# Moving the evacuation of an attention accumulator from the end of a step to its middle

## The chip, the core and the metric

The kernel runs on one core of a Trainium2 chip. The metric is the device time of one execution in microseconds (us). The engines are named as the profile names them: PE is TensorE (PEld its weight loads), ACT is ScalarE, DVE is VectorE, POOL is GpSimd, SP is SyncE, which issues the DMAs.

## The reference

It is one inference step of a two-layer encoder for a prompt of 2048 tokens and a sample of 64, at a width of 1024. Both layers have the form h + RMSNorm(W_out(gated mixer(RMSNorm(h)))). Layer 0 mixes by latent attention and by a banded attention; the change does not touch it. Layer 1 is a sliding-window attention with 16 query heads and 2 key heads of 64, in chunks of 64 tokens: a chunk reads itself and the two chunks before it, and each head has a sink logit in its softmax.

```python
def _c_layer(h, pos, cache, pre_g, post_g, w_in, sinks, w_out):
    ...
    q = _rope(q.reshape(b, s, C_HEADS, C_HEAD_DIM), pos, C_ROT).reshape(b, s, C_KV_HEADS, C_GROUP, C_HEAD_DIM)
    ...
        o = _band_prompt(q, k, v, C_PAST_CHUNKS, C_SCALE, sinks=sinks)
    ...
    return h + _rms((o * jax.nn.silu(g)) @ w_out, post_g), state
```

## The kernel before

Values are kept as pairs of a rounded high part and a remainder, so that a product of two is three matmuls; a *remainder* below is the DVE operation of `lo_of` (L214), which subtracts the high part from the PSUM source. It always follows the ACT copy of `copy` (L211), which makes the high part.

Five phases follow each other; `phase5` is layer 1's attention with the output projection. Its prompt part has 16 blocks of 128 queries, and each block has four **units**: (g, e) for key head g and parity e, with four query heads each. The units are worked by a loop over `step(n)`, which has three of them in hand at once. It takes the exponentials of unit n+1 (L1702 on ACT), starts the scores of unit n+2 (L1690 on PE, row maxima with the mask in L1693 on DVE), then for each of the (at most two) key blocks b of unit n transposes the probabilities (`turn`, L1711 on PE, into a tile `t` of `ps_t`, which has two buffers), copies them to `PT` (L211 on ACT), pumps the output projection of finished blocks (L964 on PE, into the only buffer of `ps_p`), and takes the remainder (L214 on DVE), which frees `t`. In the pass b = 0, behind that, it issues the value products of unit n-1 (`av`, L1718 on PE): four matmuls into `acc`, the only buffer of the pool `ps_o`. At the end of the step unit n-1 is evacuated by `out`:

```python
if (g, e) == (0, 0):
    while J.open >= 2:
        J.rest()
        pump(1)
    J.open += 1
    B.OT = ot.tile([128, 8, 128], F32, name="OT", bufs=2)
tbm = sc.tile([64, 512], F32, name="tbm", bufs=2)
copy(tbm, self.acc[64:128])
nc.vector.tensor_tensor(B.OT[e * 64:e * 64 + 64, g * 4:g * 4 + 4].rearrange("p j q -> p (j q)"),
                        self.acc[0:64], tbm, op=ALU.add)
if (g, e) == (1, 1):
    ...
    nc.vector.reciprocal(ri, B.rs)
    J.side.add(gate(B.OT, ri, B.i * 128, 128))
```

The accumulator's upper half is copied by ACT (`tbm`, L211) and added to its lower half by DVE (L1808); the next unit's products may start only then. For a block's first unit, `out` first lets at most one earlier block be open: its loop calls `J.rest()` and pumps the projection until that block's `gate` is through. `gate` runs beside the steps as a generator. It multiplies OT by the transposed reciprocals of the row sums (L1740 on PE, L1742 on DVE), by the gate (L1748 on POOL), copies the result to `MM` (L211 on ACT) and takes its remainder (L1755 on POOL, the last reader of OT, which has two buffers). `J.rest()` also drives the tails of the projection: DVE scales z by the row's norm and a gain (L995), POOL adds the residual (L1003).

For the first 8 steps a scheduler orders all engines. From n = 8 (about 2343 us of the profiled execution) the queues of PE, DVE, ACT and SP keep the order in which the code issues; POOL's order is still the scheduler's.

Of the kernel before, what the change touches and what calls it, by code (L numbers as in the profile page):

```python
# [110 lines left out]
def kernel(ctx, tc, a, o, upto=5):  # L111
# [1540 lines left out]
    def phase5():  # L1652

        with ExitStack() as st:
# [213 lines left out]
            def pump(rate):  # L1868
                if J.mm:
                    return J.pump(rate)  # L1870
                for _ in range(RATEL):
                    if next(left, left) is left:
                        return open_projections()
# [8 lines left out]
            def step(n):  # L1882
                cur, prv, nxt = us.get(n), us.get(n - 1), us.get(n + 1)
                if nxt:
                    nxt.exp([0, 1, 2, 3])
                if n + 2 < len(units):
                    us[n + 2] = Unit(*units[n + 2])
                    us[n + 2].start()
                    if n % 4 == 1 and n // 4 + 2 < 16:
                        blocks[n // 4 + 2] = Block(BLOCKS5[n // 4 + 2])  # L1890
                for b in range(2):
                    low = None
                    if cur and b < cur.B.nb:
                        PT, low = cur.turn(b * 128, 128)
                        cur.tasks.append(PT)
                    pump(RATE5 / 2)
                    if low:
                        low()
                    if b == 0 and prv:
                        prv.av()  # L1900
                if prv:
                    prv.out()
                    us.pop(n - 1)
                    if n % 4 == 0 and n // 4 + 1 in blocks and n > 0:
                        blocks[n // 4 + 1].load_values()
                if not J.loaded:
                    J.load.pump(1)
                if n >= NS5:
                    J.samp.pump(1)
                if J.made < FAST5:  # L1910
                    J.side.pump(SP5)
                J.rest()

            for n in range(NAUTO5):
                step(n)
            with manual(M5, ORDERED | {mybir.EngineType.SP}):
                for n in range(NAUTO5, len(units) + 1):
                    step(n)
                J.banks += [(ps_t, "t"), (ps_o, "acc")]
                J.dense = True  # L1920
                while J.done < 17:
                    J.side.pump(TAIL)
                    J.samp.pump(1)
                    J.rest()
                    J.last = J.done == 16
                    J.pump(4)
                J.side.drain()
                J.tails.drain()
# [104 lines left out]
```

## Time and profile before

| | |
|---|---|
| three timed runs | 2724.87, 2735.03, 2735.82 us (median 2735.03) |
| profiled execution | 2728.87 us, of which the span is 2727.1 |
| mean granted PE clock | 0.988 |
| last slices, PE busy of 40 us: 2400 to 2440 / 2560 to 2600 / 2600 to 2640 | 38.47 / 38.47 / 39.01 us |
| DVE busy in the same | 33.68 / 34.96 / 34.33 us |
| ACT busy in the same | 33.03 / 31.40 / 30.82 us |
| matmul L1718, mean of one | 401 ns |

A row of the timeline has its start in us from the span's start, its length in us, the engine, the line, the operation, what it writes and reads (128x512 is partitions by elements), and how many instructions of a kind were merged into it. A bracket tells how long the engine stood idle before it, and which operation ended that. In a row of groups, the busy time in us and the mean in ns stand behind the first bar, the idle time and what ended it behind the second.

### The profile page before, as it was taken

The numbers are of one execution on the slowest core, as the hardware profiler recorded it, in microseconds if no ns is written. First come the engines' busy times: TensorE is split into PE (matmuls) and PEld (weight loads), VectorE is DVE, ScalarE is ACT, GpSimd is POOL, SyncE is SP. The second block draws the span as 40 slices with busy tenths as digits, with TensorE's granted clock in tenths as the row PEclk, the third lists the DMA queues.
The fourth block names the chain that finished last, engine by engine and source line by source line (L and its number), as shares of the span: only waits on it lengthen the run. The fifth ranks groups of instructions, "written<-read, shape, count | busy, mean of one in ns | idle before, by whom it ended". The sixth has DMA issues, their size and how long they took to land. (4 is left out here: it accounts for less than half of the span.)

```text
span 2727.1 us, 46654 instructions
## 1 busy us (share of the span) xinstructions
PE 2566.5 (94%) x16296; PEld 2337.6 (86%) x16296; DVE 1568.7 (58%) x4255; ACT 1392.4 (51%) x3548; POOL 522.1 (19%) x1110
## 2 busy tenths in 40 slices
PE   7999999999999999999888999799999999999997
PEld 6999999899988888888777887679999998787886
DVE  5453345352237778787667766466223214787886
ACT  4332232422337777777666665452233223877783
POOL 0001000001002323211101333342001000344443
PEclk9999999999999999999999999999999998999999
DMA  7546444727447666651666766466425428455552
GB/s 239 171 147 209 133 143 129 255 96 234 143 118 200 194 170 188 167 155 48 194 187 167 204 191 172 149 216 224 149 96 169 127 72 246 109 139 133 137 132 70
DMA packets 382282, 437.92 MB, mean 161 GB/s; under 512 B 49936, under 2 KB 308888, under 8 KB 378816
## 3 DMA queue, kind: packets, MB, share of 16 engines
q1 hardware_dynamic: 382048, 434.95, 54.2%
q8 instruction: 129, 2.11, 0.3%
q14 instruction: 105, 0.86, 0.1%
HBM read 282.80 MB, written 157.09 MB: 161 GB/s over the span
## 5 line engine op out<-in xcount | busy, mean ns | idle before, releaser
L237 PE MATMUL pm<-X,W 128*128 128x384 f32 (+2 forms) x4536 | 752.8, 324 | 2.5 <-DVE ev L214 1.7
L237 PEld LDWEIGHTS pm<-X,W 128*128 128x128 f32 x4536 | 730.4, 189 | 6.2 <-DVE ev L214 2.3
L211 ACT ACTIVATE PT<-t 128x512 fp32r<-128x512 f32 (+3 forms) x704 | 344.5, 504 | 268.9 <-PE t L1203 113.6
L214 DVE SCALAR_TENSOR_TENSOR PT<-t,PT 128x512 fp32r<-128x512 f32 (+3 forms) x688 | 376.0, 569 | 100.8 <-ACT PT L211 99.3
L964 PE MATMUL proj<-Wo,MM 128*128 128x512 f32 (+1 forms) x1416 | 391.6, 407 | 11.3 <-ACT z L211 8.1
L964 PEld LDWEIGHTS proj<-Wo,MM 128*128 128x128 f32 (+1 forms) x1416 | 246.1, 187 | 59.5 <-ACT z L211 11.6
L214 DVE SCALAR_TENSOR_TENSOR ev<-pm,ev 128x256 fp32r<-128x256 f32 (+3 forms) x197 | 98.6, 502 | 336.9 <-ACT ev L430 102.2
L237 PE MATMUL pm<-W,X 128*128 128x256 f32 (+5 forms) x2040 | 281.2, 297 | 0.0
L237 PEld LDWEIGHTS pm<-W,X 128*128 128x128 f32 (+1 forms) x2040 | 272.0, 187 | 1.0
L702 ACT ACTIVATE P<-s,m 128x512 f32<-128x512 f32 (+9 forms) x344 | 209.3, 616 | 33.3 <-DVE m L691 30.7
L683 PE MATMUL s<-KA,Q 128*128 128x512 f32 (+7 forms) x640 | 201.1, 396 | 10.5 <-ACT P L702 8.4
L228 DVE TENSOR_TENSOR W<-R,W 128x768 fp32r<-128x768 f32 (+3 forms) x114 | 116.0, 1055 | 134.0 <-ACT W L227 133.7
L726 PE MATMUL t<-ident,P 128*128 128x128 f32 x1088 | 176.3, 276 | 3.4 <-ACT P L702 1.0
L689 DVE TENSOR_REDUCE m<-s 128x1 f32<-128x480 f32 (+7 forms) x216 | 132.4, 613 | 80.3 <-PE s L683 79.9
L726 PEld LDWEIGHTS t<-ident,P 128*128 128x128 f32 x1088 | 134.6, 141 | 41.7 <-ACT P L702 15.1
L754 PE MATMUL acc<-PT,V 128*128 128x256 f32 x1152 | 156.3, 285 | 6.6 <-DVE OT L763 6.6
L754 PEld LDWEIGHTS acc<-PT,V 128*128 128x128 f32 x1152 | 140.6, 188 | 12.0 <-PE t L726 6.0
L1702 ACT ACTIVATE P<-s,m 128x256 f32<-128x256 f32 (+2 forms) x264 | 119.4, 465 | 11.6 <-DVE m L1694 10.3
L1216 PE MATMUL acc<-PT,V 128*128 128x256 f32 x672 | 111.6, 298 | 13.7 <-DVE OT L1226 11.0
L1180 DVE CUSTOM_DVE_ANT_0 s<-s,bias 128x640 f32<-128x640 f32 (+4 forms) x128 | 95.4, 745 | 42.9 <-PE s L1176 40.7
L1693 DVE CUSTOM_DVE_ANT_0 s<-s,mask 128x256 f32<-128x256 f32 (+1 forms) x256 | 107.6, 422 | 20.2 <-PE t L1711 10.9
L683 PE MATMUL s<-KR,Q 128*128 128x384 f32 (+6 forms) x320 | 116.2, 363 | 0.6 <-DMA Q<-sQR 0.6
(248 smaller groups left out, 3927.7 us busy)
## 6 DMA issues: line engine op xcount, KB each, us to landing
Q<-sQA SPq DMA_DIRECT2D x128, 128.0 KB, 3.3
sWO<-W SPq DMA_DIRECT2D x32, 512.0 KB, 3.8
Q<-sQB SPq DMA_DIRECT2D x128, 128.0 KB, 3.1
Wo<-sWO SPq DMA_DIRECT2D x16, 1024.0 KB, 8.8
Q<-sQC SPq DMA_DIRECT2D x32, 512.0 KB, 7.7
R<-in_ab_w_in_dram SPq DMA_DIRECT2D x40, 384.0 KB, 4.1
K<-sKB SPq DMA_DIRECT2D x56, 256.0 KB, 5.6
V<-sVB SPq DMA_DIRECT2D x24, 512.0 KB, 6.7
```

Of the source, the lines that this page charges most:

```text
L211: nc.scalar.activation(out, in_, AF.Copy)
L214: nc.vector.scalar_tensor_tensor(out, x, scale, hi, op0=ALU.mult, op1=ALU.subtract)
L228: nc.vector.tensor_tensor(Wv[:, 1, k0:k1], Rv, Wv[:, 0, k0:k1], op=ALU.subtract)
L237: nc.tensor.matmul(ps, lhs(x, k), rhs(y, k), start=(j == 0), stop=(j == n - 1))
L683: nc.tensor.matmul(s[:r, :n], self.Q[:, x, self.qo:self.qo + r], rhs, start=(x == 0), stop=(x == 2))
L689: nc.vector.tensor_reduce(m[:r, j:j + 1], s[:r, :n], axis=AX.X, op=ALU.max)
L702: nc.scalar.activation(self.P[:r, o0:o0 + n], self.s.pop(j)[:r, :n], AF.Exp, bias=self.m[:r, 6:7], accum_out=acc)
L726: nc.tensor.transpose(t[:, b], self.P[:, (b0 + b) * 128:(b0 + b + 1) * 128], ident)
L754: nc.tensor.matmul(acc[:, (i // 2) % 2], H.V[:, b0 + b], PT[:, x, b], start=(b0 + b == 0 and x == 0), stop=(b0 + b == i and x == 1))
L964: nc.tensor.matmul(p, M[:, x, k, :r], W[k][:, y, cs], start=(k == k0 and t == 0), stop=(k == k1 - 1 and t == 2))
L1216: nc.tensor.matmul(acc, self.H.V[:, self.base - self.H.b0 + b], self.PT[:, x, off + b], start=(b == 0 and x == 0), stop=(b == nblk - 1 and ...
L1702: nc.scalar.activation(self.P[:, c, :w], self.s[:, c, :w], AF.Exp, bias=m[:, 1, c:c + 1], accum_out=m[:, 0, c:c + 1])
```

## The change

The call of `out` moves from the step's end into the pass b = 0, directly behind `av`. With it move the loop of a block's first unit, the reciprocal, and the start of `gate` of its last.

```diff
                         low()
                     if b == 0 and prv:
                         prv.av()
+                        prv.out()
                 if prv:
-                    prv.out()
                     us.pop(n - 1)
                     if n % 4 == 0 and n // 4 + 1 in blocks and n > 0:
                         blocks[n // 4 + 1].load_values()
```

The order of the built programs differs only from step 8 on. SP's order is the same throughout, and POOL's main operations keep theirs but for small ones on row sums.

*The step that evacuates a block's last unit (1, 1).* On DVE, between the row maxima of the unit started and the first operation of `gate` of the block before, there stood before:

```order
L1694 SCALAR_TENSOR_TENSOR m<-m,nsink 128x4
L214 SCALAR_TENSOR_TENSOR PT<-t,PT 128x512 x2
L1808 TENSOR_TENSOR OT<-acc,tbm 64x512
L1812 RECIPROCAL ri<-rsum 128x16
L1742 TENSOR_TENSOR OT<-OT,t 128x512
```

And now:

```order
L1694 SCALAR_TENSOR_TENSOR m<-m,nsink 128x4
L214 SCALAR_TENSOR_TENSOR PT<-t,PT 128x512
L1808 TENSOR_TENSOR OT<-acc,tbm 64x512
L1812 RECIPROCAL ri<-rsum 128x16
L214 SCALAR_TENSOR_TENSOR PT<-t,PT 128x512
L1742 TENSOR_TENSOR OT<-OT,t 128x512
```

The addition and the reciprocal now stand between the two remainders.

*The same step and the next on ACT.* The first two rows of PT belong to the closing unit's step; behind the exponentials (L1702) begins the step that evacuates the next block's first unit (0, 0). Before:

```order
L211 ACTIVATE PT<-t 128x512 x2
L211 ACTIVATE z<-proj 128x512
L211 ACTIVATE tbm<-acc 64x512
L1702 ACTIVATE P,m<-s,m 128x256 x4
L1705 ACTIVATE m<-m 128x4
L211 ACTIVATE PT<-t 128x512
L983 ACTIVATE sq,ss_27397<-z 128x512
L211 ACTIVATE PT<-t 128x512
L211 ACTIVATE MM<-OT 128x1024
L211 ACTIVATE tbm<-acc 64x512
```

And now:

```order
L211 ACTIVATE PT<-t 128x512
L211 ACTIVATE tbm<-acc 64x512
L211 ACTIVATE PT<-t 128x512
L211 ACTIVATE z<-proj 128x512
L1702 ACTIVATE P,m<-s,m 128x256 x4
L1705 ACTIVATE m<-m 128x4
L211 ACTIVATE PT<-t 128x512
L983 ACTIVATE sq,ss_27397<-z 128x512
L211 ACTIVATE MM<-OT 128x1024
L211 ACTIVATE tbm<-acc 64x512
L211 ACTIVATE PT<-t 128x512
```

In the first step tbm passes one copy of PT and that of z; in the second, tbm and the copy of MM pass the second copy of PT.

*The step that evacuates a block's first unit (0, 0).* On DVE, from the end of the row maxima of this step to the first of the next, before:

```order
L1694 SCALAR_TENSOR_TENSOR m<-m,nsink 128x4
L214 SCALAR_TENSOR_TENSOR PT<-t,PT 128x512 x2
L995 SCALAR_TENSOR_TENSOR z<-z,rs,g_post 128x512 x2
L1808 TENSOR_TENSOR OT<-acc,tbm 64x512
L1693 ISA s,m<-s,mask 128x256
```

And now:

```order
L1694 SCALAR_TENSOR_TENSOR m<-m,nsink 128x4
L214 SCALAR_TENSOR_TENSOR PT<-t,PT 128x512
L995 SCALAR_TENSOR_TENSOR z<-z,rs,g_post 128x512 x2
L1808 TENSOR_TENSOR OT<-acc,tbm 64x512
L214 SCALAR_TENSOR_TENSOR PT<-t,PT 128x512
```

The second remainder is now behind the pair of L995 and the addition. On PE the loop's two groups of projection products go along:

```order
 L1718 MATMUL acc<-PT,VC 128x512 x4
-L1711 MATMUL t<-ident,P 128x128 x4
 L964 MATMUL proj<-Wo_25852,MM 128x512 x3
 L964 MATMUL proj<-Wo_25854,MM 128x512 x3
+L1711 MATMUL t<-ident,P 128x128 x4
 L964 MATMUL proj<-Wo_26273,MM 128x512 x3
 L964 MATMUL proj<-Wo_26275,MM 128x512 x3
```

There the second transpositions stand behind two more groups of projection products. This is PE's only difference, in twelve such steps; a first unit with only one key block (query block 0) has no second transpositions.

## The prediction

> **What bounds the kernel now.** I read the page's busy shares first, then the window of layer 1's attention grouped by line, then the timelines of TensorE and of all engines over one block.
>
> ```profile
> span 2727.1 us, 46654 instructions
> PE 2566.5 (94%) x16296; PEld 2337.6 (86%) x16296; DVE 1568.7 (58%) x4255; ACT 1392.4 (51%) x3548; POOL 522.1 (19%) x1110
> ```
>
> TensorE (PE) is busy for 94% of the span; only time in which it waits can be won. The next rows are PE's groups of 2343 to 2680 us, where the order of layer 1's steps is written by hand: count, busy time, mean, then the idle time before the group and who ended it.
>
> ```profile
> L964 PE MATMUL proj<-Wo,MM 128*128 128x512 f32 x639 | 171.0, 406 | 0.0
> L1711 PE MATMUL t<-ident,P 128*128 128x128 f32 x432 | 65.5, 275 | 2.3 <-DVE PT L214 1.1
> L1718 PE MATMUL acc<-PT,VC 128*128 128x512 f32 x216 | 60.7, 401 | 13.0 <-DVE OT L1808 13.0
> ```
>
> The value products (L1718) alone wait: 13.0 us, for the addition L1808 that empties their only accumulator. Is this spread over all steps? PE's timeline says no:
>
> ```profile
> 2383.57 0.66 PE L1711 MATMUL t<-ident,P 128*128 128x128 f32 x4 [1.09 <-DVE PT L214]
> 2405.09 1.16 PE L1718 MATMUL acc<-PT,VC 128*128 128x512 f32 x4 [0.56 <-DVE OT L1808]
> 2429.45 1.17 PE L1718 MATMUL acc<-PT,VC 128*128 128x512 f32 x4 [0.71 <-DVE OT L1808]
> 2453.81 1.17 PE L1718 MATMUL acc<-PT,VC 128*128 128x512 f32 x4 [0.71 <-DVE OT L1808]
> 2503.81 1.22 PE L1718 MATMUL acc<-PT,VC 128*128 128x512 f32 x2 [3.80 <-DVE OT L1808]
> 2673.03 1.16 PE L1718 MATMUL acc<-PT,VC 128*128 128x512 f32 x4 [1.65 <-DVE OT L1808]
> 2685.87 5.81 PE L964 MATMUL acc<-Wo,MM 128*128 128x512 f32 x24 [1.65 <-DVE OT L1808]
> ```
>
> It comes once in a block of four steps, 24.36 us apart (2429.45 to 2453.81), always after the **opening** step, which evacuates a block's first unit. The step before it, which evacuates the last unit of the block before, I call **closing**; the one after it, **following**. This is an opening step, then the following one, on all engines:
>
> ```profile
> 2420.75 0.63 DVE L1742 TENSOR_TENSOR OT<-OT,t 128x512 f32<-128x512 f32 x1
> 2421.46 2.40 POOL L1748 TENSOR_TENSOR OT<-OT,G 128x1024 f32<-128x1024 f32 x1 [4.18 <-DVE OT L1742]
> 2423.80 1.43 DVE L214 SCALAR_TENSOR_TENSOR PT<-t,PT 128x512 fp32r<-128x512 f32 x2
> 2423.91 0.60 ACT L211 ACTIVATE PT<-t 128x512 fp32r<-128x512 f32 x1 [0.93 <-PE t L1711]
> 2424.40 1.05 ACT L211 ACTIVATE MM<-OT 128x1024 fp32r<-128x1024 f32 x1
> 2425.15 3.56 DVE L995 SCALAR_TENSOR_TENSOR z<-z,rs,g_post 128x512 f32<-128x512 f32 x2
> 2425.53 2.63 POOL L1755 TENSOR_TENSOR MM<-OT,MM 128x1024 fp32r<-128x1024 f32 x1 [1.37 <-ACT MM L211]
> 2428.63 0.67 DVE L1808 TENSOR_TENSOR OT<-acc,tbm 64x512 f32<-64x512 f32 x1
> 2429.23 0.41 DVE L1693 CUSTOM_DVE_ANT_0 s<-s,mask 128x256 f32<-128x256 f32 x1
> 2430.81 1.19 PE L1690 MATMUL s<-KC,Q 128*128 128x256 f32 x8
> 2431.39 1.28 DVE L214 SCALAR_TENSOR_TENSOR PT<-t,PT 128x512 fp32r<-128x512 f32 x2
> 2432.14 0.66 PE L1711 MATMUL t<-ident,P 128*128 128x128 f32 x4
> ```
>
> The addition is late because VectorE (DVE) is: it works without a pause from L1742 to the remainders (L214) of 2431.39. Two things lengthen that stretch. First, the pair of L995 takes 3.56 us, where one usually takes 0.74:
>
> ```profile
> L995 DVE SCALAR_TENSOR_TENSOR z<-z,rs,g_post x26: 732/743/2903, 2376.0 to 2669.4; 128x512 f32<-128x512 f32 x24, 64x512 f32<-64x512 f32 x2
> 2503.07 0.68 DVE L1808 TENSOR_TENSOR OT<-acc,tbm 64x512 f32<-64x512 f32 x1 [4.79 <-POOL MM L1755]
> ```
>
> The second L995 stands still until GpSimd's L1755 ends (2428.16) and is done 0.55 later. Second, the addition needs L1755 itself, as the row of 2503.07 shows: it frees the OT buffer. So the chain of an opening step is L1742, L1748, the copy of MM, L1755, L1808; then the row maxima (L1693) and the remainder at 2431.39. That remainder is a second wait: the following step's transpositions start at 2432.14, 0.14 after the scores end (2430.81 + 1.19 = 2432.00), and need its t buffer.
>
> **The change part by part.** No instruction is added or taken out, and SP's queue is the same, so no transfer moves. What moves is the accumulator's copy (tbm, ScalarE), the addition, a closing step's reciprocal, and in an opening step two groups of projection products, now ahead of the second transpositions. All that PE does is still done: 0 us in itself.
>
> *Closing step.* These are its rows, one block later than above:
>
> ```profile
> 2440.71 1.08 PE L1718 MATMUL acc<-PT,VC 128*128 128x512 f32 x4
> 2441.63 0.60 PE L1711 MATMUL t<-ident,P 128*128 128x128 f32 x4
> 2442.27 0.60 ACT L211 ACTIVATE PT<-t 128x512 fp32r<-128x512 f32 x1 [2.14 <-PE t L1711]
> 2442.90 0.69 DVE L214 SCALAR_TENSOR_TENSOR PT<-t,PT 128x512 fp32r<-128x512 f32 x1 [0.95 <-ACT PT L211]
> 2442.97 0.60 ACT L211 ACTIVATE z<-proj 128x512 f32<-128x512 f32 x1
> 2443.59 0.59 ACT L211 ACTIVATE tbm<-acc 64x512 f32<-64x512 f32 x1
> 2444.16 0.60 PE L1711 MATMUL t<-ident,P 128*128 128x128 f32 x4
> 2444.22 0.68 DVE L1808 TENSOR_TENSOR OT<-acc,tbm 64x512 f32<-64x512 f32 x1 [0.63 <-ACT tbm L211]
> 2444.94 0.26 DVE L1812 RECIPROCAL ri<-rsum 128x16 f32<-128x16 f32 x1
> ```
>
> The products end at 2441.79; ScalarE and DVE then idle (2.14, 0.95, 0.63) for transpositions and for a copy that stands third in its queue. In the new order tbm runs at 2441.88 (an estimate: 0.09 behind the products) to 2442.47, the second PT copy to 2443.10, the addition 2442.51 to 2443.2, the reciprocal to 2443.4, the remainder 2443.4 to 2444.1. L1742 starts at 2444.05, not at 2420.75 + 24.36 = 2445.11: **1.06 us earlier** against PE. The remainder now ends at 2444.1 instead of 2443.59 and frees the buffer for transpositions at 2444.16: 0.06 are left, cost 0.
>
> *Opening step.* L1748 ends 1.06 earlier. The copy of MM no longer stands behind the second PT copy, which held it from 2423.86 to 2424.40; taking 0.50, L1755 and the addition come **1.56** earlier, at 2427.07 on the clock above. But the second remainder is now behind the addition instead of ahead of L995: +0.65 (half of 1.28). So maxima, first remainder and buffer come 1.56 - 0.65 = **0.91** earlier. The products of the following step need that second remainder only for their fourth matmul, some 0.9 us in, when it is done. The two projection groups ahead of the second transpositions cost nothing: those transpositions' PT copy and remainder are behind tbm and the addition anyhow.
>
> What does PE lose there now? Where it doesn't wait, it overlaps neighbours:
>
> ```profile
> 2432.55 2.35 PE L964 MATMUL proj<-Wo,MM 128*128 128x512 f32 x9
> 2434.73 1.10 PE L1718 MATMUL acc<-PT,VC 128*128 128x512 f32 x4
> 2443.13 1.19 PE L1690 MATMUL s<-KC,Q 128*128 128x256 f32 x8
> ```
>
> Products start 0.17 before the projection's end, transpositions 0.16 before the scores' (2444.16 against 2444.32). So an opening costs 0.71 + 0.17 at the products and 0.14 + 0.16 at 2432.14, or 1.18 us; 1.05 if the first overlap is left out. DVE gives back 0.91 of it; 0.1 to 0.3 stays as a wait of L1711 for L214.
>
> Whether the second L995 still runs into L1755 hardly matters. L1755 would be issued at 2448.33, the pair at 2447.78 and 2448.45, so the race is 0.12 us from turning; if the second wins, L1755 ends at 2451.6 and the addition starts at 2451.65 instead of 2451.45. [...]
>
> *The sum.* Thirteen openings stand in 2343 to 2680. Ten are like the one above (0.56 to 0.81 at the products): 10 x 0.91 = 9.1. The first, whose 1.09 at 2383.57 waits for the same remainder: 0.9. That of 2503.81 has no second remainder, but no second PT copy to be rid of either: 1.06 to 1.5, taken 1.3. The last (1.65) has no maxima behind it: 1.5. The end (1.65 at 2685.87) waits for a tbm that now stands ahead of a z copy: 1.3. Together **14.1 us**. The profiled execution took 2728.87 us (span 2727.1), so 2714.8. The three timed runs are 2724.87, 2735.03 and 2735.82; their median lies 6.2 above the profiled one, which puts the same gain at 2720.9. I forecast **2717**, between the two.
>
> Bounds. The idle times set the most: 12 x 1.18 + 3.8 + 1.65, about 19.5. The least, if DVE's stretch starts no earlier: 0.50 - 0.65, below nothing, taken 0 per block.
>
> **The rivals.**
> *All of it is won.* If DVE comes early enough for both waits, 19.5 go: 2709. For it: the residue is only 0.1 to 0.3. Against: the work on DVE between L1755's end and the transpositions grows by one remainder.
> *The wait changes its name.* If L1742 is not earlier (because ScalarE is not free at 2441.88), only the 0.50 of MM's copy is won and 0.65 paid; products no longer wait, the following transpositions do, by what was saved. 2729, no change. For it: DVE has no pause in the stretch. Against: the idle 2.14, 0.95 and 0.63 of the closing step, just where the moved pair lands.
> *Slower.* DVE and ScalarE take their instructions in order, so the closing step's second remainder must wait for tbm and the addition. If tbm starts as late as now, the addition at 2444.22 and the reciprocal put the remainder at 2445.1 to 2445.8, and the opening step's transpositions 1.7 us behind 2444.16. Against the 1.05 it replaces that is +0.7 in 12 blocks: 2737. It decides from a tbm 1 us later than worked out (0.06 + 0.91). [...]
>
> **How the numbers follow.** Forecast 0.55, all of it 0.10, changed name 0.27, slower 0.08. The range runs from 2706 (all of it, from the fastest timed run: 2724.87 - 19.5 = 2705.4) to 2730 (no change). About 0.5%, or 13.7 us, is what a measurement of this kernel can tell from no change, so faster means under 2721.4: most of the forecast case and all of the first rival, less what runs that differ by 11 us blur: 0.53. Same 0.42; slower 0.05, the worse part of the last rival with that blur.
>
> **What would show it.** Right: the products' wait for L1808 falls from 13.0 to under 4 us, the block's period from 24.36 to about 23.45, ACT's rows read tbm between two PT copies, L1755 starts 1.5 us earlier against PE. A new wait of L1711 for L214 of 0.1 to 0.3 a block is expected; 0.7 or more means the second rival; waits before the opening step's transpositions mean the third. Wrong altogether: waits in steps that have none now, or a z copy (L211) that PE starts to wait for.

## The result and the profile after

| | before | after |
|---|---|---|
| median of five runs | 2735.03 us (2724.87 to 2735.82) | 2710.89 us (2704.74 to 2715.87) |
| ratio, 95% interval | | 0.992 [0.9894, 0.9947] |
| span of the profiled execution | 2727.1 us | 2704.2 us |
| period of a block of four steps | 24.35 us | 23.11 us |

The change makes the kernel faster by 0.8%. In a second comparison, together with experiments, the changed kernel stood at 0.9932 [0.9915, 0.9948]. This is the head of the page of after, with the busy shares of the engines:

```profile
span 2704.2 us, 46634 instructions
PE 2562.3 (95%) x16296; PEld 2337.8 (86%) x16296; DVE 1568.3 (58%) x4255; ACT 1390.6 (51%) x3548; POOL 520.4 (19%) x1110
```

The work is the same. PE's busy time is 4.2 us shorter (2566.5 to 2562.3) and the span 22.9 us, so most of what has gone is waiting. PE's groups of 2343 to 2660 us in after (behind the last bar the idle time and what ended it):

```profile
L1711 PE MATMUL t<-ident,P 128*128 128x128 f32 x428 | 64.8, 274 | 0.4 <-DVE PT L214 0.4
L1718 PE MATMUL acc<-PT,VC 128*128 128x512 f32 x212 | 58.0, 393 | 2.4 <-DVE OT L1808 2.4
```

The products waited 13.0 us for the addition; 2.4 are left. The transpositions waited 2.3; 0.4 are left. PE's timeline in after has only these waits for the evacuation in the steps in question:

```profile
2379.34 0.66 PE L1711 MATMUL t<-ident,P 128*128 128x128 f32 x4 [0.38 <-DVE PT L214]
2493.32 0.74 PE L1718 MATMUL acc<-PT,VC 128*128 128x512 f32 x2 [2.36 <-DVE OT L1808]
2663.09 5.80 PE L964 MATMUL acc<-Wo,MM 128*128 128x512 f32 x24 [0.27 <-DVE OT L1808]
```

The 0.7 us that stood in every block are gone without a successor. The timeline of all engines in after, a closing step and the opening step behind it, shows how:

```profile
2411.04 1.08 PE L1718 MATMUL acc<-PT,VC 128*128 128x512 f32 x4
2412.22 0.59 ACT L211 ACTIVATE tbm<-acc 64x512 f32<-64x512 f32 x1 [1.77 <-PE acc L1718]
2412.84 0.68 DVE L1808 TENSOR_TENSOR OT<-acc,tbm 64x512 f32<-64x512 f32 x1 [0.56 <-ACT tbm L211]
2413.71 0.63 DVE L214 SCALAR_TENSOR_TENSOR PT<-t,PT 128x512 fp32r<-128x512 f32 x1
2414.26 0.68 DVE L1742 TENSOR_TENSOR OT<-OT,t 128x512 f32<-128x512 f32 x1
2415.01 2.41 POOL L1748 TENSOR_TENSOR OT<-OT,G 128x1024 f32<-128x1024 f32 x1 [3.05 <-DVE OT L1742]
2417.03 1.09 PE L1718 MATMUL acc<-PT,VC 128*128 128x512 f32 x4
2417.45 1.06 ACT L211 ACTIVATE MM<-OT 128x1024 fp32r<-128x1024 f32 x1 [0.51 <-POOL OT L1748]
2417.96 3.60 DVE L995 SCALAR_TENSOR_TENSOR z<-z,rs,g_post 128x512 f32<-128x512 f32 x2
2418.59 2.42 POOL L1755 TENSOR_TENSOR MM<-OT,MM 128x1024 fp32r<-128x1024 f32 x1 [0.86 <-ACT MM L211]
2421.48 0.67 DVE L1808 TENSOR_TENSOR OT<-acc,tbm 64x512 f32<-64x512 f32 x1
2423.22 1.08 PE L1718 MATMUL acc<-PT,VC 128*128 128x512 f32 x4
2424.84 0.68 DVE L214 SCALAR_TENSOR_TENSOR PT<-t,PT 128x512 fp32r<-128x512 f32 x1
2425.58 0.66 PE L1711 MATMUL t<-ident,P 128*128 128x128 f32 x4
```

Read it from the opening step's products (2417.03 here, 2422.35 before). L1755 starts 1.56 us behind them; before it was 3.18 (2425.53). The addition starts 4.45 behind them; before, 6.28. The next products (2423.22) come 1.07 us after the addition's end (2422.15), so they no longer feel it. The first remainder of the following step starts 7.81 behind them (2424.84), where it was 9.04, and the transpositions that need it (2425.58) run through.

The period can be read from the reciprocals (L1812), one in each block. Five blocks in before, then five in after:

```profile
2542.42 0.25 DVE L1812 RECIPROCAL ri<-rsum 128x16 f32<-128x16 f32 x1
2664.17 0.25 DVE L1812 RECIPROCAL ri<-rsum 128x16 f32<-128x16 f32 x1
```

```profile
2527.69 0.25 DVE L1812 RECIPROCAL ri<-rsum 128x16 f32<-128x16 f32 x1
2643.22 0.25 DVE L1812 RECIPROCAL ri<-rsum 128x16 f32<-128x16 f32 x1
```

121.75 / 5 = 24.35 and 115.53 / 5 = 23.11: **1.24 us a block**. Of the 22.9 us of the span, 2.95 stand ahead of the part with the written order, where both programs are alike: the last addition ahead of it stands at 2340.90 in before and at 2337.95 in after. That is scatter between executions. The change itself is worth the other 20 us in this pair, some 1.3 of them by TensorE's clock (last section).

### The profile page after: what moved, and what is told of

Read it like the earlier page. It is cut to its first block, busy times and chain, and to the rows that moved or that the text cites. A ratio compares the mean times of both kernels' runs of the same rounds, so it can differ in the third digit from the quotient of the medians.

```text
span 2704.2 us, 46634 instructions
## 1 busy us (share of the span) xinstructions
PE 2562.3 (95%) x16296; PEld 2337.8 (86%) x16296; DVE 1568.3 (58%) x4255; ACT 1390.6 (51%) x3548; POOL 520.4 (19%) x1110
## 5 line engine op out<-in xcount | busy, mean ns | idle before, releaser
L214 DVE SCALAR_TENSOR_TENSOR PT<-t,PT 128x512 fp32r<-128x512 f32 (+3 forms) x688 | 377.2, 568 | 78.4 <-ACT PT L211 77.2
L964 PE MATMUL proj<-Wo,MM 128*128 128x512 f32 (+1 forms) x1416 | 396.6, 410 | 10.7 <-ACT z L211 8.1
L964 PEld LDWEIGHTS proj<-Wo,MM 128*128 128x128 f32 (+1 forms) x1416 | 248.6, 188 | 58.6 <-ACT z L211 11.3
L214 DVE SCALAR_TENSOR_TENSOR ev<-pm,ev 128x256 fp32r<-128x256 f32 (+3 forms) x197 | 98.6, 503 | 338.3 <-ACT ev L430 101.1
L1702 ACT ACTIVATE P<-s,m 128x256 f32<-128x256 f32 (+2 forms) x264 | 119.3, 471 | 8.8 <-DVE m L1694 8.7
L1693 DVE CUSTOM_DVE_ANT_0 s<-s,mask 128x256 f32<-128x256 f32 (+1 forms) x256 | 107.8, 422 | 19.6 <-PE t L1711 8.5
```

Source lines behind the costliest of these rows:

```text
L214: nc.vector.scalar_tensor_tensor(out, x, scale, hi, op0=ALU.mult, op1=ALU.subtract)
L964: nc.tensor.matmul(p, M[:, x, k, :r], W[k][:, y, cs], start=(k == k0 and t == 0), stop=(k == k1 - 1 and t == 2))
L1702: nc.scalar.activation(self.P[:, c, :w], self.s[:, c, :w], AF.Exp, bias=m[:, 1, c:c + 1], accum_out=m[:, 0, c:c + 1])
```

## The experiments

The change touches all four units of a block. Which of them counts? Three theories stood at first. A: DVE's long stretch starts earlier because the *closing* unit is evacuated earlier. B: what counts is the earlier evacuation of the *opening* unit. C: each step brings its own share. Four kernels evacuate only some units in the middle of their steps:

```diff
+EARLY = ((1, 1),)
...
                     if b == 0 and prv:
                         prv.av()
+                        if (prv.g, prv.e) in EARLY:
+                            prv.out()
                 if prv:
-                    prv.out()
+                    if (prv.g, prv.e) not in EARLY:
+                        prv.out()
```

With these four, the lines behind the edit have numbers one higher (L1719 are the products, L1809 the addition, L1712 the transpositions, L215 the remainder, L1743, L1749 and L1756 the gate's three operations, L996 the z pair).

**The closing unit alone**, `EARLY = ((1, 1),)`:

> Only a block's last unit (1, 1) is evacuated in the middle of its step; the other three stay at the end. Theory A (VectorE's stretch from the gate's first product L1742 to the next remainder is the bound, and the closing step makes it start earlier): L1742 about 1.2 us earlier against PE, the block's period falls from 24.36 to 23.1-23.3 us, the time by 14-19 us against before. Theory B (PE waits for the accumulator of the block's first unit, so it is that unit's earlier evacuation that counts): period stays at 24.3-24.4, time within 3 us of before. Theory C (each of the four steps gives its share): period about 24.05, 4-6 us.

2724.63 us (2719.22 to 2733.28), ratio 0.9991 [0.9975, 1.0007] against 2729.11 of before. Period 24.35, the products still wait 0.7 in each ordinary block. Theory A is wrong as it stands. Its timeline over an opening step tells why:

```profile
2422.94 0.68 DVE L1743 TENSOR_TENSOR OT<-OT,t 128x512 f32<-128x512 f32 x1
2423.69 2.40 POOL L1749 TENSOR_TENSOR OT<-OT,G 128x1024 f32<-128x1024 f32 x1 [3.05 <-DVE OT L1743]
2425.71 1.09 PE L1719 MATMUL acc<-PT,VC 128*128 128x512 f32 x4
2427.27 0.60 ACT L212 ACTIVATE PT<-t 128x512 fp32r<-128x512 f32 x1 [1.66 <-PE t L1712]
2427.77 1.05 ACT L212 ACTIVATE MM<-OT 128x1024 fp32r<-128x1024 f32 x1
2428.90 2.62 POOL L1756 TENSOR_TENSOR MM<-OT,MM 128x1024 fp32r<-128x1024 f32 x1 [2.49 <-ACT MM L212]
2432.81 1.17 PE L1719 MATMUL acc<-PT,VC 128*128 128x512 f32 x4 [0.70 <-DVE OT L1809]
```

L1743 is earlier, by as much as with the full change: 2.77 us ahead of the products, not 1.60. L1749 is done at 2426.09. But the copy of MM stands in ScalarE's queue behind the second PT copy, which waits for PE's second transpositions (1.66) and runs at 2427.27. MM starts at 2427.77, 2.06 behind the products, as before (2424.40 - 2422.35 = 2.05). POOL idles instead (2.49), and nothing reaches PE. Two places outside the ordinary blocks gain: the long wait (3.80 in before) falls to 2.36, in a step without a second PT copy, and the wait at the end falls from 1.65 to 0.28. These 2.8 us are less than the comparison can tell from nothing.

**The opening unit alone**, `EARLY = ((0, 0),)`:

> Only a block's first unit (0, 0) is evacuated in the middle of its step. Theory A: the copy of MM gains 0.5 us, the remainder behind the addition costs 0.6, so the period stays within 0.15 us of 24.36 and the time within 4 us of before; the wait at the products gets shorter and one at the following transpositions longer. Theory B: period 23.1-23.5, 12-19 us faster. Theory C: about 24.05, 4-6 us.

2726.32 us (2721.77 to 2733.01), ratio 1.0 [0.9985, 1.0015]. Here the wait does change its name. From its timeline:

```profile
2420.29 1.09 PE L1719 MATMUL acc<-PT,VC 128*128 128x512 f32 x4
2422.99 2.42 POOL L1756 TENSOR_TENSOR MM<-OT,MM 128x1024 fp32r<-128x1024 f32 x1 [0.86 <-ACT MM L212]
2425.88 0.67 DVE L1809 TENSOR_TENSOR OT<-acc,tbm 64x512 f32<-64x512 f32 x1
2426.60 1.20 PE L1719 MATMUL acc<-PT,VC 128*128 128x512 f32 x4
2429.23 1.28 DVE L215 SCALAR_TENSOR_TENSOR PT<-t,PT 128x512 fp32r<-128x512 f32 x2
2429.97 0.66 PE L1712 MATMUL t<-ident,P 128*128 128x128 f32 x4 [0.78 <-DVE PT L215]
```

L1756 starts 2.70 behind the products instead of 3.18, and the addition 5.59 instead of 6.28: the products no longer wait. But the second remainder now runs behind the addition, so the next step's first remainder starts at 8.94 instead of 9.04, and the transpositions wait 0.78 for it. Period 24.25.

**The two middle units alone**, `EARLY = ((0, 1), (1, 0))`, and **all but the opening one**, `EARLY = ((0, 1), (1, 0), (1, 1))`:

> Only the units (0, 1) and (1, 0) are evacuated in the middle of their steps. Theories A and B: no wait of PE lies there, period 24.3-24.4, time within 3 us of before. Theory C: about 23.7, 8-11 us faster.

> All units but a block's first (0, 0) are evacuated in the middle. Theory A: like the closing unit alone, period 23.1-23.2, time within 3 us of the changed kernel. Theory B: period 24.3-24.4, time like before. Theory C: about 23.4.

2728.93 us, ratio 1.0003 [0.9988, 1.0018], and 2725.21, ratio 0.9992 [0.9978, 1.0006]. Both keep the wait of 0.7 in each block and the period of 24.35 (24.34 for the first). Theories A, B and C all fall: in an ordinary block no part has a share that could be added.

**A fourth theory, D.** The rows of the first two runs suggest two gates in a row. The copy of MM starts behind the *later* of two things: the end of L1748, which the closing part brings forward, and the second PT copy, which the opening part takes out of the way. L1755 follows 1.13 us after its start. The next four kernels try this. In two of them, only the loop of `out` moves, without the accumulator's copy and addition:

```diff
-                def out(self):
+                def room(self):
                     B, g, e = self.B, self.g, self.e
                     if (g, e) == (0, 0):
                         while J.open >= 2:
...
+                def out(self):
+                    B, g, e = self.B, self.g, self.e
                     tbm = sc.tile([64, 512], F32, name="tbm", bufs=2)
...
                     if b == 0 and prv:
                         prv.av()
+                        prv.room()
```

The kernel of the closing unit and the loop has `if (prv.g, prv.e) == (1, 1): prv.out()` below that line as well. In both, the addition is L1811. The first of the four below is the earlier edit with `EARLY = ((0, 0), (1, 1))`.

> Only the opening and the closing units are evacuated in the middle of their steps; the other two units of a block at the end, as before. Theory D (two gates in a row: GpSimd's MM remainder starts 1.1 us behind the later of the gating product's end and of the second PT copy; the closing part brings the first earlier, the opening part takes the second away, and either alone leaves the other standing): the whole gain, period 23.1 us as with the full change, 2704 to 2714 us, no wait of the products for the addition. Theory F (the four units of a block each empty the accumulator earlier, and it takes all four to let TensorE run through): the middle units are missing, so a wait of 0.5 us or more stays in each block, period above 23.8, 2718 to 2726 us.

> The closing unit is evacuated in the middle of its step; of the opening unit only the loop that waits for an open block moves there, which puts the copy of MM ahead of the second PT copy on ScalarE. Its tbm copy and its addition stay at the step's end, and the second remainder now stands behind the pair of z on DVE, ahead of the addition. Theory D: the MM remainder starts as early as with the full change; the addition ends 0.65 us later than there, which the 1.07 us that it has to spare before the next products cover; period 23.1 (23.0 to 23.3), 2704 to 2714 us. Theory E (what counts in the opening step is that its own accumulator is copied and added in the middle): no better than the closing part alone, wait of the products 0.6 to 0.8 in each block, period 24.35, 2722 to 2728 us.

> Of the opening unit only the loop that waits for an open block moves to the middle of the step (copy of MM ahead of the second PT copy); all accumulators are evacuated at the end of their steps, as before. Theory D: the gating product is no earlier, so the MM remainder gains 0.5 to 0.7 us, and the second remainder, now behind the pair of z, puts 0.65 back on the addition: wait of the products 0.5 to 0.8 in each block, period 24.2 to 24.4, 2722 to 2729 us. If the second PT copy alone were what held the chain: period below 23.6, 2708 to 2717 us.

> The full change, on the same chip as the three others: 2704 to 2714 us, period 23.1. All theories expect the same; it is the measure for the other three.

| kernel | median us | ratio to before (2730.27), 95% |
|---|---|---|
| closing and opening unit | 2712.30 (2708.48 to 2717.80) | 0.9937 [0.9922, 0.9952] |
| closing unit and loop | 2712.96 (2710.45 to 2718.26) | 0.9941 [0.9928, 0.9955] |
| loop alone | 2727.02 (2720.30 to 2733.82) | 0.9992 [0.9978, 1.0006] |
| the full change | 2713.94 (2703.99 to 2714.92) | 0.9932 [0.9915, 0.9948] |

The timeline of the loop alone:

```profile
2425.70 1.09 PE L1718 MATMUL acc<-PT,VC 128*128 128x512 f32 x4
2428.39 2.42 POOL L1755 TENSOR_TENSOR MM<-OT,MM 128x1024 fp32r<-128x1024 f32 x1 [0.86 <-ACT MM L211]
2431.89 0.67 DVE L1811 TENSOR_TENSOR OT<-acc,tbm 64x512 f32<-64x512 f32 x1
2432.71 1.17 PE L1718 MATMUL acc<-PT,VC 128*128 128x512 f32 x4 [0.64 <-DVE OT L1811]
```

And of the closing unit with the loop:

```profile
2424.94 1.09 PE L1718 MATMUL acc<-PT,VC 128*128 128x512 f32 x4
2425.38 1.06 ACT L211 ACTIVATE MM<-OT 128x1024 fp32r<-128x1024 f32 x1 [0.51 <-POOL OT L1748]
2426.52 2.43 POOL L1755 TENSOR_TENSOR MM<-OT,MM 128x1024 fp32r<-128x1024 f32 x1 [0.86 <-ACT MM L211]
2430.02 0.67 DVE L1811 TENSOR_TENSOR OT<-acc,tbm 64x512 f32<-64x512 f32 x1
2431.14 1.08 PE L1718 MATMUL acc<-PT,VC 128*128 128x512 f32 x4
2432.78 1.28 DVE L214 SCALAR_TENSOR_TENSOR PT<-t,PT 128x512 fp32r<-128x512 f32 x2
```

The kernels that matter, with times in us behind the start of the opening step's products, each from one opening step of its timeline:

| kernel | end of L1748 | start of L1755 | addition | next first remainder | period |
|---|---|---|---|---|---|
| before | 1.51 | 3.18 | 6.28 | 9.04 | 24.35 |
| closing unit alone | 0.38 | 3.19 | 6.28 | 9.05 | 24.35 |
| loop alone | 1.52 | 2.69 | 6.19 | 8.95 | 24.26 |
| opening unit alone | 1.52 | 2.70 | 5.59 | 8.94 | 24.25 |
| closing unit and loop | 0.40 | 1.58 | 5.08 | 7.84 | 23.20 |
| closing and opening unit | 0.39 | 1.56 | 4.46 | 7.82 | 23.20 |
| the full change | 0.39 | 1.56 | 4.45 | 7.81 | 23.11 |

Theory D holds in every row: L1755 moves by 0.00, by 0.49 and, with both, by 1.60, and the period falls by more than 0.1 only with both. With the loop alone, the second remainder, now behind the pair of z, puts back on the addition nearly all of the 0.49 (6.28 to 6.19). The loop also moves the pair of z and two groups of projection products, and no kernel moves the copy of MM by itself. That the copy is the piece that counts is read from the rows: wherever the loop has moved, it starts 0.03 to 0.04 behind the end of L1748.

The last three rows also show what does not count. The addition 0.63 us later (5.08 against 4.45) costs nothing in an ordinary block, because there is a margin of 1.07 behind it (in the last opening a wait of 0.46 stays): theory E, that the opening accumulator itself must be emptied in the middle, is wrong. Theory F, that it takes all four units, is wrong too; the middle units bring the 0.09 a block between 23.20 and 23.11 at most. The pair of z takes 3.6 us in all of them, with and without a gain.

The times of the three kernels with both parts cannot be told apart. The largest wait left is that of 2.36 at 2493.32. POOL's timeline in after shows the residual addition ahead of L1755 in that block:

```profile
2487.85 2.39 POOL L1003 TENSOR_TENSOR x<-z,x 128x1024 f32<-128x1024 f32 x1 [1.72 <-DVE z L995]
2490.20 2.35 POOL L1755 TENSOR_TENSOR MM<-OT,MM 128x1024 fp32r<-128x1024 f32 x1
```

L1755 ends at 2492.55, and the addition and the products follow. Another order of the two was not tried; the 2.4 us are 0.09% of the time, less than these comparisons tell from nothing.

## Why the prediction was right, and where its sizes were off

The forecast of 2717 lay on the right side, the measured 2710.89 within the range. That alone says little, as the range reached from the first rival to no change, and how near the two numbers come is in part scatter: before has medians of 2735.03, 2729.11 and 2730.27 in its three comparisons, and the medians of before and after differ by 24.1 us in the first and by 16.3 in the last. So the pieces count, as the prediction put them:

*Closing step.* tbm was to start 0.09 behind the products' end; it starts 0.10 behind (2411.04 + 1.08 = 2412.12; 2412.22). L1742 was to be 1.06 earlier against PE; it is 1.18 earlier (3.22 behind the closing products instead of 4.40). Right, a little too small. The third rival, a late tbm, did not come. That DVE and ScalarE keep the order of their queues, on which it rested, these runs do show: L1693 starts at 2429.23 in before, behind the addition, though its scores end at 2427.62, and with the closing unit alone the copy of MM starts at 2.06 though its input is there at 0.38.

*Opening step.* L1755 was to start 1.56 earlier; it is 1.62 (3.18 to 1.56). Right. The sum of 1.06 and 0.50 was right too, but it read like two shares. The single runs show that in an ordinary block the 1.06 alone is worth nothing and the 0.50 alone next to nothing.

*The addition.* This is the term that was mis-sized: it comes 1.83 earlier, not 1.56, since L1755 itself is shorter as well (2.42 instead of 2.63). It now starts 0.63 behind the pair of z, not 0.38 (2418.59 - 2417.96; 2425.53 - 2425.15); that this is what shortens it is not shown. With the second remainder behind the addition (0.60 lost, 0.65 expected) the next first remainder gains 1.23 instead of **0.91**.

*PE's loss.* 1.18 a block were there to be won, with the overlaps (without the 0.17 it is 1.01, not the 1.05 of the prediction). DVE gives back 1.23, so all of it is won, and the wait of L1711 for L214, expected to stay at 0.1 to 0.3, does not appear in the ordinary blocks (0.38 is left behind the first opening). The period fell to 23.11, not 23.45. In size, then, the first rival ("all of it is won", chance 0.10) is what happened, by the forecast's steps.

*The second rival* ("the wait changes its name") described exactly the kernel with the opening unit alone: L1711 waits 0.78 there. It was not what the full change does, for the reason that the prediction gave: the closing step's idle times let L1742 come earlier.

*The rest of the sum.* The gain of a piece is how much earlier the same products start in after than in before: 2.95 us ahead of the first opening, 22.78 at the end (2685.87 - 2663.09). Ten blocks gave 12.2 instead of 9.1, the first opening 1.3 instead of 0.9, the last 2.2 instead of 1.5 (its 1.65, a wait of 0.18 in the next step, and overlaps), the end 1.4 instead of 1.3 (a wait of 1.65 that fell to 0.27). The block of 2503.81 was put at 1.3. Its wait fell by 1.44 (3.80 to 2.36), but the two blocks around it show more. The reciprocals there, in before and then in after:

```profile
2469.27 0.25 DVE L1812 RECIPROCAL ri<-rsum 128x16 f32<-128x16 f32 x1
2518.08 0.25 DVE L1812 RECIPROCAL ri<-rsum 128x16 f32<-128x16 f32 x1
```

```profile
2459.75 0.25 DVE L1812 RECIPROCAL ri<-rsum 128x16 f32<-128x16 f32 x1
2504.59 0.25 DVE L1812 RECIPROCAL ri<-rsum 128x16 f32<-128x16 f32 x1
```

48.81 - 44.84 = 3.97; less one ordinary block (1.24), 2.73. Of these, 1.44 are the wait; the other 1.3 are put down to TensorE's clock, which the prediction left out (last section): from the products behind the wait to the projection that follows, 3.26 us pass in before (2503.81 to 2507.07, clock 0.50 until 2506.89) and 1.88 in after (2493.32 to 2495.20, clock 1.00). The kernel with the closing and the opening unit, whose wait is 2.38 where that of after is 2.36, has a half clock there; after has none. The sum is 12.2 + 1.3 + 2.7 + 2.2 + 1.4 = 19.8, against 20 measured and 14.1 predicted. The prediction's upper bound of 19.5 was added up wrongly: its own rows give eleven openings at 1.18 (the ten and the first), the 3.8 and two waits of 1.65, or 20.1.

*The race* of the second L995 against L1755 stayed as it was, by less than the 0.12 worked out: L1755 starts at 2418.59 and the second L995 at 2418.62, and the pair takes 3.60. The second L995 ends 0.55 us behind L1755 (2421.01 and 2421.56), as it did in before. What the other order costs was the author's estimate; before has it once, where an L995 starts at 2401.22, 0.10 ahead of L1755, and takes 0.74 while L1755 takes 2.90 instead of 2.63.

## What to carry to other kernels

When an operation waits for the later of two things that are freed by different edits, each edit alone can measure as nothing: look at every queue between the piece that came earlier and the engine that should feel it, before an edit is written off. With the closing unit alone, the copy of MM stood in ScalarE's queue behind a copy that waited for another engine, and inherited that wait, whatever its own input did (the input was there at 0.38 and the copy started at 2.06). And an earlier time is worth something only as far as the next instruction still waits: the addition could be 0.63 us later here at no cost.

## What the runs showed of the hardware

In seven of the ten profiled executions TensorE's granted clock is halved for 3.41 us at the end of the long wait of this part or up to 1.5 us behind it; in three it is not. Windows of the timeline (length, then the engines' busy times; the last three columns are granted clock, DMA share, GB/s) in before, behind its wait of 3.80:

```profile
2504.50:2505.50 1.00, 1.00 (x6) 0.90 (x5) 0.93 (x5) 0.43 (x1) 0.00 (x0) 0.50 0.02 8
```

In the kernel with the closing and the opening unit, behind a wait of 2.38 (2494.09):

```profile
2496.00:2497.00 1.00, 1.00 (x6) 0.90 (x5) 0.93 (x4) 0.99 (x4) 0.20 (x1) 0.50 0.00 0
2497.00:2498.00 1.00, 1.00 (x4) 0.81 (x3) 0.93 (x4) 1.00 (x6) 0.02 (x1) 0.50 0.52 123
```

And in after, behind a wait of 2.36:

```profile
2493.30:2495.50 2.20, 2.18 (x15) 2.07 (x16) 2.06 (x10) 1.41 (x4) 0.12 (x1) 1.00 0.48 188
2495.50:2498.50 3.00, 3.00 (x14) 2.44 (x13) 2.83 (x10) 2.99 (x12) 1.37 (x8) 1.00 0.46 175
```

Nine matmuls (L964) take 3.52 us in the second and 2.35 in the last: 1.17 us more behind one wait of 2.4 us than behind another.

In the clock records of before and of after, all changes of the granted clock inside the span lie whole multiples of 3.413 us apart, and each stretch of half clock that ends inside it lasts 3.41, 6.83 or 10.24 us. For each kernel, this is the long wait, how much of it lies in the 3.41 us just ahead of the half clock, and the clock that follows:

| kernel | long wait, us | of it in the 3.41 us ahead of the half clock, us | clock that follows |
|---|---|---|---|
| before | 3.80 | 3.41 | 0.50 |
| middle units alone | 3.78 | 2.89 | 0.50 |
| closing unit and loop | 2.35 | 2.35 | 0.50 |
| loop alone | 3.85 | 2.00 | 0.50 |
| opening unit alone | 3.85 | 1.98 | 0.50 |
| closing and opening unit | 2.38 | 1.95 | 0.50 |
| all but the opening unit | 2.35 | 1.88 | 0.50 |
| the full change (first trace) | 2.36 | no half clock | 1.00 |
| the full change (second trace) | 2.37 | no half clock | 1.00 |
| closing unit alone | 2.36 | no half clock | 1.00 |

Six waits of nearly one length, 2.35 to 2.38 us, gave both outcomes. With the opening unit alone, the other 1.87 us of the wait lay ahead of those 3.41 us, and the clock stayed full behind them (1.00 from 2498.00 to 2501.10). In after, counted on in steps of 3.413 us from its other changes of the clock, the wait is cut into 0.88 and 1.48 us, and the clock is 1.00 from 2491.84 to 2498.67. Elsewhere in before the half clock begins at 2305.50 behind 3.41 us in which PE is idle for 0.76, and the clock is full behind 3.41 us with 1.88 idle (1854.95 to 1858.36). What decides the outcome is not shown.

The waits of 0.7 in the ordinary blocks show no such dip: the clock is 1.00 there (2429 to 2433 in before).
